# Gates of both layers and the even layer's queries and keys computed by token and turned by 16-bit DMA transposes

## The chip, the cores and the metric

The kernel runs on one core of a Trainium2 chip. A core has five engines, each of which works off its own queue of instructions in order: TensorE (PE in the profile; PEld is its weight loading), VectorE (DVE), ScalarE (ACT), GpSimd (POOL) and SyncE (SP), which here only issues DMAs. Sixteen DMA engines move the data. The metric is the device time of one execution in microseconds (us), the median over several runs.

## The reference, cut to what matters

Two residual layers work on 256 tokens of width 2048; a last RMS norm follows. Each layer normalises, projects, attends in sixteen heads of 128 features, multiplies by a SiLU gate, projects back and adds.

```python
for layer in (even_layer, odd_layer):
    x = x + layer(rms_norm(x, g_layer))
return rms_norm(x, g_final)

def even_layer(y):
    qa, ka, va, ga, qb, kb, vb, gb = _split(y @ w_in, EVEN_SPLITS)
    oa = dilated_attention(qa, ka, va, bias_a)
    ob = neighbourhood_attention(qb, kb, vb, rpb_b)
    mix = concatenate([oa * silu(ga), ob * silu(gb)])
    return mix @ w_out
```

The odd layer has the same frame. Its heads C (eight, with a sink logit) have queries, two key and value heads and gates; its heads D (eight) normalise and rotate queries and keys, and have two key and value heads too. The logits of a head are the product of its queries and keys over the 128 features, so both are wanted with the features on the partitions.

## The kernel before

Every float32 product is made of three products of halves, hi x hi, hi x lo and lo x hi, summed in PSUM. The input `X` lies in SBUF as 16 slices of 128 features, each split into hi and lo. The weights are 268 tiles of 128x1024 (512 KB), read once each in the order of the list `plan`. The class `Weights` (L54 to L74) loads a tile into one of five raw buffers (L65, issued by SyncE), ScalarE casts it to `whi` (L69) and VectorE makes the rest `wlo` (L70); there are three pairs of `whi` and `wlo`. `weights()` (L78) keeps two tiles ahead of TensorE.

A unit of work is a group of weight tiles that share one result in PSUM. It has two forms.

- By feature (L275): the weights are stationary and the input streams through. A tile holds four slices of 256 features; each slice takes two matmuls of 512 columns (L284) and two of 256 (L288). A unit is four tiles and gives 256 features, features on the partitions. To evict it ScalarE copies one half out of PSUM, VectorE adds the other and multiplies by the row scale of the norm, which `spread_scale` (L187) has laid along the columns.
- By token (L294): the input is stationary and the weights stream, in three matmuls a slice (`mm3`, L100). A unit is eight tiles of two slices and gives 512 features, tokens on the partitions; with 256 features it is four tiles of four slices.

Before the change the queries, keys and gates of the even layer (24 units), and the gates, the C queries and the first keys of the odd layer (13 units) are made by feature. Values and the D heads are made by token; the D heads are turned by TensorE after their rotation (`normed_rope`, L362).

The order of the work is set by Python generators. `step()` (L216) is called once a weight tile and moves each list of generators on by one: `evac` (evictions), `post` (rotation) and `bg` (attention). `attend` (L423) does two heads: logits, exponentials, the turning of the probabilities, weighing of the values, in about ten steps. The turning (L475 to L492) goes by 16-bit halves: GpSimd parts the words into halves (L480), two DMA transposes turn them (L482), GpSimd joins them (L491). DMAs given to `pinned` (L85) keep their place in program order. SyncE issues all DMAs in order, so that a DMA which waits holds up those behind it. `ROOM` (L205) says how many queries, keys, gates and bias tables may live at once. Seven constants of `load_consts` (L144) are loaded while the second pair of heads is under way. `project_out` works through the output weights by `out_order` (L561).

Of the kernel before, what the change touches and what calls it, by code (L numbers as in the profile page):

```python
# [36 lines left out]
def encoder(ctx, tc, a, out):  # L37
# [37 lines left out]

    plan, ready = [], []
# [102 lines left out]
    def row_scale(layer, parts):  # L179
# [5 lines left out]
        return r  # L185

    def spread_scale(r):  # L187
# [28 lines left out]
    def step():  # L216

        advance(evac)
        advance(post)
        attention()  # L220
# [16 lines left out]
    def drain():  # L237
        while evac or post or bg:
            step()
# [15 lines left out]
    steps = {}  # L255

    def need(pr):

        while pr not in done:
            assert evac or post or bg  # L260
# [101 lines left out]
    def normed_rope(tag, q, ss, g, scale, give):  # L362
# [21 lines left out]
        yield  # L384
        yield from room(tag)
# [7 lines left out]
        yield  # L393

# [28 lines left out]
    def attend(idx, q, kv, silu, frees, bias=None, sink=None, shared=False):  # L423

        (qh, ql), (kh, kl), (vh, vl, v0) = q, kv[0], kv[1]
# [100 lines left out]
        yield  # L526
        o = ps_o.tile([P, 2, S], F32, tag="o", name="ps_out")
# [4 lines left out]
        yield True  # L532
        m = tp.tile([P, 2, S], F32, tag="tmp", name="mx", bufs=4)
# [426 lines left out]
```

## Time and profile before

| What | Before |
|---|---|
| Median of 3 runs | 817.8 us (817.39 to 818.31) |
| Profiled execution, its span | 817.19 us, 815.4 us |
| TensorE's granted clock | 0.997 |
| TensorE busy | 805.6 us, 99% |
| VectorE, ScalarE, GpSimd busy | 577.7, 447.8, 128.6 us |
| DMA | 168.47 MB, 207 GB/s |

How to read it: matmuls overlap in the array, and the modelled end of one lies beyond the start of the next, so the duration of a matmul is not what it costs; its cost is read from start to start in the timeline. Idle time of an engine that nobody waits for costs nothing. A wait for several things is put down to the one that ended last.

### The profile page before, as it was taken

What the parts mean: (1) busy time and instruction counts of PE and PEld (TensorE: products, weight loads), DVE (VectorE), ACT (ScalarE), POOL (GpSimd) and SP (SyncE); (2) the same over time, 40 slices, a digit from 0 to 9 for tenths busy, and PEclk for the clock granted to TensorE, in tenths of its full rate; (3) what the DMA queues carried; (4) which work ended last, traced back from release to release, by engine and by line L of the source; (5) the groups of instructions that cost most, each with busy time, mean ns of one, the idle gap of its engine ahead of it and who ended that gap; (6) DMA issues with size and microseconds to landing.
All of it is one profiled execution on the core that took longest, in us unless ns stands there. A gap on an engine that the chain in (4) does not pass through costs nothing.

```text
span 815.4 us, 11762 instructions
## 1 busy us (share of the span) xinstructions
PE 805.6 (99%) x4293; PEld 691.7 (85%) x4293; DVE 577.7 (71%) x855; ACT 447.8 (55%) x712; POOL 128.6 (16%) x100
## 2 busy tenths in 40 slices
PE   9999999999999999999999999999999999999996
PEld 7888888888888888888888888888889888888885
DVE  6677676677857887497656776685987776765863
ACT  7755454555545554455445555657656665664651
POOL 0002020021302240040204300002112223221000
PEclk9999999999999999999999999999999999999998
DMA  9957675565755756566758755566558676767632
GB/s 337 362 200 221 250 228 181 207 206 175 235 176 171 231 164 245 186 186 222 203 184 194 253 198 166 197 203 201 153 179 231 221 213 186 235 196 227 206 133 103
DMA packets 97066, 168.47 MB, mean 207 GB/s; under 512 B 55472, under 2 KB 56368, under 8 KB 96944
## 3 DMA queue, kind: packets, MB, share of 16 engines
q1 hardware_dynamic: 96864, 167.71, 64.3%
q8 instruction: 33, 0.54, 0.3%
q14 instruction: 25, 0.20, 0.1%
q10 hardware_dynamic: 144, 0.02, 0.0%
HBM read 155.64 MB, written 3.05 MB: 195 GB/s over the span
## 4 chain that ended last, share of the span: by engine, by line
PE 98%; DMA 1%; DVE 0%; SPq 0%; ACT 0%; issue 0%; ACTq 0%; DVEq 0%
PE ps_f L284 34%; PE ps_f L288 17%; PE ps_t L103 14%; PE ps_t L104 14%; PE ps_t L102 13%; PE ps_s L104 1%; PE ps_s L103 1%; PE ps_s L102 1%; PE ps_out L103 1%; PE ps_out L102 1%; PE ps_out L104 1%; DMA wraw<-in_even_t 1%; SPq L87 0%; PE ps_tr L389 0%; DVE wlo L70 0%; ACT whi L69 0%
## 5 line engine op out<-in xcount | busy, mean ns | idle before, releaser
L70 DVE TENSOR_TENSOR wlo<-wraw,whi 128x1024 fp32r<-128x1024 f32 (+1 forms) x270 | 346.3, 1283 | 184.6 <-ACT whi L69 183.3
L69 ACT CAST whi<-wraw 128x1024 fp32r<-128x1024 f32 (+1 forms) x270 | 282.2, 1045 | 300.2 <-PE ps_t L104 127.8
L284 PE MATMUL ps_f<-x,whi 128*128 128x512 f32 x1184 | 372.1, 396 | 0.0
L288 PEld LDWEIGHTS ps_f<-x,wlo 128*128 128x128 f32 x1184 | 222.2, 188 | 53.5 <-DVE wlo L70 1.2
L288 PE MATMUL ps_f<-x,wlo 128*128 128x256 f32 x1184 | 233.0, 278 | 0.0
L284 PEld LDWEIGHTS ps_f<-x,whi 128*128 128x128 f32 x1184 | 180.8, 189 | 0.5
L102 PE MATMUL ps_t<-whi,x 128*128 128x512 f32 (+1 forms) x256 | 96.3, 379 | 0.6 <-ACT x L95 0.5
L103 PE MATMUL ps_t<-wlo,x 128*128 128x512 f32 (+1 forms) x256 | 96.1, 377 | 0.1
L104 PE MATMUL ps_t<-whi,x 128*128 128x512 f32 (+1 forms) x256 | 95.9, 377 | 0.0
L480 POOL COPY ph<-pr 128x1024 uint16<-128x1024 uint16 x32 | 39.5, 1235 | 350.8 <-ACT pr L470 182.9
L102 PE MATMUL ps_t<-whi,mh 128*128 128x512 f32 x240 | 93.5, 389 | 0.0
L103 PE MATMUL ps_t<-wlo,mh 128*128 128x512 f32 x240 | 93.5, 389 | 0.0
L104 PE MATMUL ps_t<-whi,ml 128*128 128x512 f32 x240 | 93.4, 389 | 0.0
L491 POOL COPY pt<-pa 128x1024 uint16<-128x1024 uint16 x32 | 51.5, 1608 | 35.8 <-DMA pa<-ph 35.8
L102 PEld LDWEIGHTS ps_t<-whi,x 128*128 128x128 f32 x256 | 48.2, 188 | 9.6 <-ACT x L95 1.3
L104 PEld LDWEIGHTS ps_t<-whi,x 128*128 128x128 f32 x256 | 48.2, 188 | 9.0 <-DVE x L96 0.2
L103 PEld LDWEIGHTS ps_t<-wlo,x 128*128 128x128 f32 x256 | 48.2, 189 | 8.6 <-DVE wlo L70 0.5
L104 PEld LDWEIGHTS ps_t<-whi,ml 128*128 128x128 f32 x240 | 45.1, 188 | 9.3
L102 PEld LDWEIGHTS ps_t<-whi,mh 128*128 128x128 f32 x240 | 45.1, 188 | 9.2
L103 PEld LDWEIGHTS ps_t<-wlo,mh 128*128 128x128 f32 x240 | 45.1, 188 | 9.1
L420 POOL TENSOR_TENSOR bias<-maskB,rpb 128x512 f32<-128x512 f32 x8 | 12.2, 1526 | 137.6 <-DMA rpb<-rows 137.6
L462 ACT ACTIVATE pr<-lg,mn 128x256 f32<-128x256 f32 (+1 forms) x48 | 24.0, 501 | 16.8 <-POOL ph L480 9.2
(133 smaller groups left out, 675.5 us busy)
## 6 DMA issues: line engine op xcount, KB each, us to landing
wraw<-in_even_f SPq DMA_DIRECT2D x96, 512.0 KB, 3.4
wraw<-in_odd_f SPq DMA_DIRECT2D x56, 512.0 KB, 3.6
wraw<-in_w_out_even SPq DMA_DIRECT2D x32, 512.0 KB, 4.1
wraw<-in_w_out_odd SPq DMA_DIRECT2D x32, 512.0 KB, 4.2
wraw<-in_even_t SPq DMA_DIRECT2D x30, 512.0 KB, 4.3
wraw<-in_odd_t SPq DMA_DIRECT2D x24, 512.0 KB, 3.4
xraw<-in_xt SPq DMA_DIRECT2D x8, 256.0 KB, 7.0
h<-in_x SPq DMA_DIRECT2D x4, 512.0 KB, 8.6
```

The source lines that it names most:

```text
L69: nc.scalar.copy(self.hi[:, c], raw[:, c])
L70: nc.vector.tensor_sub(self.lo[:, c], raw[:, c], self.hi[:, c].bitcast(F32))
L102: nc.tensor.matmul(dst, lh, rh, start=first, stop=False, skip_group_check=True)
L103: nc.tensor.matmul(dst, lh, rl, start=False, stop=False, skip_group_check=True)
L104: nc.tensor.matmul(dst, ll, rh, start=False, stop=last, skip_group_check=True)
L284: nc.tensor.matmul(acc[:, f, :], w.hi[:, c], xx[k], start=k == 0, stop=False, skip_group_check=True)
L288: nc.tensor.matmul(acc[:, f, :S], w.lo[:, c], xh[k], start=False, stop=k == KC - 1, skip_group_check=True)
L420: nc.gpsimd.tensor_tensor(b, maskB.unsqueeze(1).to_broadcast([P, 2, S]), raw, op=ALU.subtract)
L462: nc.scalar.activation(p[:, t, :W], lg[:, t, :W], AF.Exp, bias=mn[:, t : t + 1], scale=-1.0, accum_out=den[:, t : t + 1],)
L480: nc.gpsimd.tensor_copy(halves, words)
L491: nc.gpsimd.tensor_copy(words.bitcast(U16).rearrange("p c (q s) -> p s c q", s=2), st[i])
```

## The change

Queries and keys of the even layer, the gates of both layers, and the first keys of the odd layer are computed by token, 512 features a unit; the first odd keys share a unit with the first odd values. `side_by_side` fills a weight tile from two groups of 256 features: two DMAs, each with two runs of 1 KB a partition. `EVEN` gives the order of the even units: a digit is queries and keys of one pair of heads, `g` the gates of two pairs, `v` their values.

ScalarE scales the pieces by the row scale while it copies them from PSUM (`evict_turned`, `evict_gates`). GpSimd parts the words into halves, two DMA transposes turn them, GpSimd joins them; queries and keys are then split into hi and lo. For gates, Tanh and the product come before the turning, and the joined words are the gate. The queues `later` and `jobs` are moved on by `step()`. Attention begins when the keys are given, and waits for values and gates where it uses them. The spread scale stays for the C queries alone, which are still made by feature.

```diff
+            if isinstance(src, list):
+                for place, piece in src:
+                    nc.sync.dma_start(place(raw), piece)
             for i, c in enumerate(cols):
                 load = nc.sync.dma_start if x is None else pinned
-                load(raw[:, c], src[:, c])
+                if not isinstance(src, list):
+                    load(raw[:, c], src[:, c])
...
+    def side_by_side(left, right):
+        for j in range(NJ):
+            pieces = []
+            for i, group in enumerate((left, right)):
+                place = lambda raw, i=i: raw.rearrange("p (k c) -> p k c", k=KK)[:, :, i * S : (i + 1) * S]
+                src = group[j // 2].rearrange("p (k c) -> p k c", c=S)
+                pieces.append((place, src[:, j % 2 * KK : (j % 2 + 1) * KK]))
+            plan.append((pieces, None))
...
+        half, minus = [const.tile([P, 2], F32, tag=f"{x}{layer}", name=f"{x}{layer}") for x in ("half", "minus")]
+        nc.vector.tensor_scalar_mul(half, r, 0.5)
+        nc.vector.tensor_scalar_mul(minus, r, -SCALE)
+        return r, half, minus
...
-        rk = const.tile([P, S], F32, tag="rk", name="rk")
         rq = const.tile([P, S], F32, tag="rq", name="rq")
-        nc.vector.tensor_copy(rk, bc)
-        nc.vector.tensor_scalar_mul(rq, rk, -SCALE)
-        rhalf = const.tile([P, S], F32, tag="rhalf", name="rhalf")
-        nc.vector.tensor_scalar_mul(rhalf, rk, 0.5)
-        return rk, rq, rhalf
-    evac, post, bg, done = [], [], [], set()
+        nc.vector.tensor_scalar_mul(rq, bc, -SCALE)
+        return rq
...
+        turn(later)
+        turn(jobs)
...
-    def gate(acc, rhalf):
-        g = scaled(acc, rhalf)
-        e = tp.tile([P, 2, S], F32, tag="ge", name="ge", bufs=1)
-        nc.scalar.activation(e, g, AF.Tanh)
+    def evict_gates(acc, half, pairs):
+        for i, pr in enumerate(pairs):
+            g = tp.tile([P, 2, S], F32, tag="tmp", name="gf", bufs=4)
+            for t in range(2):
+                nc.scalar.mul(g[:, t, :], acc[t][:, i * S : (i + 1) * S], half[:, t : t + 1])
+            later.append(gate(g, pr))
+            steps[id(later[-1])] = 0
+            yield
+    def gate(g, pr):
+        e = tp.tile([P, 2, S], F32, tag="ge", name="ge")
+        tc.keep_in_program_order(nc.scalar.activation(e, g, AF.Tanh))
+        nc.vector.scalar_tensor_tensor(g, e, 1.0, g, ALU.add, ALU.mult)
+        yield
+        halves = tp.tile([P, 2, 2, S], U16, tag="ge", name="gh")
+        tc.keep_in_program_order(
+            nc.gpsimd.tensor_copy(halves, g.bitcast(U16).rearrange("p t (k s) -> p t s k", s=2))
+        )
+        yield
+        across = g.rearrange("p t k -> p (t k)").bitcast(U16).rearrange("p (s c q) -> p s c q", s=2, c=2)
+        for t in range(2):
+            pinned(
+                across[:, :, :, t * P : (t + 1) * P].rearrange("p s c q -> p (s c) q"),
+                halves[:, t].rearrange("p s k -> p (s k)"), transpose=True,
+            )
+        yield
+        yield
+        yield
+        yield from room("silu")
         s = silu_tile()
-        nc.vector.scalar_tensor_tensor(s, e, 1.0, g, ALU.add, ALU.mult)
-        return s
+        tc.keep_in_program_order(
+            nc.gpsimd.tensor_copy(s.bitcast(U16).rearrange("p c (q s) -> p s c q", s=2), across)
+        )
+        yield
+        gated[pr] = s
+        yield
+    def evict_turned(acc, parts):
+        for i, (tag, scale, give) in enumerate(parts):
+            f = tp.tile([P, 2, S], F32, tag="tmp", name="tf", bufs=4)
+            for t in range(2):
+                nc.scalar.mul(f[:, t, :], acc[t][:, i * S : (i + 1) * S], scale[:, t : t + 1])
+            jobs.append(turned(f, tag, give))
+            steps[id(jobs[-1])] = 0
+            yield
+    def turned(f, tag, give):
+        words = tp.tile([P, 2, S], F32, tag="tmp2", name="tw")
+        halves, across = [
+            x.rearrange("p t k -> p (t k)").bitcast(U16).rearrange("p (x y z) -> p x y z", x=2, y=2) for x in (words, f)
+        ]
+        pin(nc.gpsimd.tensor_copy(halves, f.bitcast(U16).rearrange("p t (k s) -> p t s k", s=2)))
+        yield
+        for t in range(2):
+            pinned(
+                across[:, :, :, t * P : (t + 1) * P].rearrange("p s c q -> p (s c) q"),
+                halves[:, t].rearrange("p s k -> p (s k)"), transpose=True,
+            )
+        yield
+        yield
+        yield
+        pin(nc.gpsimd.tensor_copy(words.bitcast(U16).rearrange("p c (q s) -> p s c q", s=2), across))
+        yield
+        yield from room(tag)
+        dst = pair(tag)
+        split(*dst, words, None, pin)
+        yield
+        give(dst)
...
+            vh, vl, v0 = kv[1]()
...
+        while held or kv[1]() is None:
+            yield
+        held.append(idx)
...
+        while idx not in gated:
+            yield True
         m = tp.tile([P, 2, S], F32, tag="tmp", name="mx", bufs=4)
-        nc.vector.tensor_mul(m, o, silu)
+        pin(nc.vector.tensor_mul(m, o, gated.pop(idx)))
...
-    def even_order(u):
-        tokens, first = [(None, "v")], [(0, "q"), (0, "k")]
-        head = tokens + first if u == 0 else first + tokens
-        return head + [(0, "g"), (1, "q"), (1, "k"), (1, "g")]
+    EVEN = ["v 0 g 1", "g 0 v 1", "g 0 v 1", "0 1 v g"]
     for u in range(4):
-        for pr, kind in even_order(u):
+        for kind in EVEN[u].split():
             if kind == "v":
                 plan.extend((a["even_t"][u][j], None if u else j) for j in range(8))
+            elif kind == "g":
+                side_by_side(a["even_f"][2 * u][2], a["even_f"][2 * u + 1][2])
             else:
-                plan.extend((a["even_f"][2 * u + pr]["qkg".index(kind)][j], None) for j in range(4))
+                side_by_side(*(a["even_f"][2 * u + int(kind)][i] for i in range(2)))
     out_plan("even")
     for t, fs in ((0, ()), (1, (10, 11)), (2, (12, 13))):
         plan.extend((a["odd_t"][t][j], None) for j in range(8))
-        plan.extend((a["odd_f"][f][j], None) for f in fs for j in range(4))
-    plan.extend((a["odd_f"][f][j], None) for f in (0, 1, 2, 6, 3, 7, 4, 8, 5, 9) for j in range(4))
+        if fs:
+            side_by_side(*(a["odd_f"][f] for f in fs))
...
+    def evict_even(u, kind, acc):
+        r, half, minus = scales[0]
         if kind == "v":
-            values(st["v"], acc, r)
-        elif kind == "q":
-            st["q"] = scaled_split("q", acc, rq)
+            tiles = values_tile()
+            values(tiles, acc, r)
+            yield
+            yield
+            v[u] = tiles
+        elif kind == "g":
+            yield from evict_gates(acc, half, (2 * u, 2 * u + 1))
+        else:
+            p, st = 2 * u + int(kind), {}
             heads = (2 * (p % 4), 2 * (p % 4) + 1)
-            st["bias"] = [bias_table(a["bias_a"][x]) if p < 4 else bias_rpb(x) for x in heads]
-        elif kind == "k":
-            st["k"] = scaled_split("k", acc, rk)
-        else:
-            s = gate(acc, rhalf)
-            v = (*st["v"], p % 2 * S)
-            bg.append(attend(p, st["q"], (st["k"], v), s, ("q", "k", "silu", "bias", "bias"), st["bias"]))
+            bias = [bias_table(a["bias_a"][x]) if p < 4 else bias_rpb(x) for x in heads]
+            def begin(dst):
+                bg.append(attend(p, st["q"], (dst, lambda: u in v and (*v[u], p % 2 * S) or None), ("q", "k", "silu", "bias", "bias"), bias))
+            yield from evict_turned(acc, [("q", minus, lambda dst: st.__setitem__("q", dst)), ("k", r, begin)])
...
+    def evict_odd(i, acc, st):
+        st["q", i] = scaled_split("q", acc, scales[1])
+        st["bias", i] = [bias_table(a["bias_c"][x]) for x in (2 * i, 2 * i + 1)]
+        yield
+        yield
+        while "k" not in st:
+            yield
+        attend_odd(0, i, st)
+        yield
+    def gate_pairs(first):
+        evac.append(evict_gates(by_token(512, token_acc()), half1, (first, first + 1)))
     st = {}
     acc = by_token(512, token_acc())
     evac += [evict_heads(st, ("k", None), acc), evict_values(part(acc, 1), 1)]
     for i in (0, 2):
         evac.append(evict_heads(st, (("q", i), ("q", i + 1)), by_token(512, token_acc())))
-        for m in range(2):
-            evac.append(evict_odd(1, "g", i + m, by_feature(), st))
+        gate_pairs(4 + i)
     st = {}
-    evac.append(evict_odd(0, "k", 0, by_feature(), st))
-    evac.append(evict_values(part(by_token(S, token_acc()), 0), 0))
+    acc = by_token(512, token_acc())
+    evac += [evict_turned(acc, [("k", r1, lambda dst: st.__setitem__("k", dst))]), evict_values(part(acc, 1), 0)]
     for i in range(4):
-        for kind in "qg":
-            evac.append(evict_odd(0, kind, i, by_feature(), st))
+        evac.append(evict_odd(i, by_feature(), st))
+        if i % 2 == 0:
+            gate_pairs(i)
```

TensorE's queue around the first logits of the even layer, before (`ps_f` is a unit by feature, `ps_s` the logits):

```order
L284 MATMUL ps_f_708<-x0_87,whi_665 128x512 x2
L288 MATMUL ps_f_708<-x0_87,wlo_666 128x256 x2
L102 MATMUL ps_s_739<-kh_634,qh_599 128x256
L103 MATMUL ps_s_739<-kl_635,qh_599 128x256
L104 MATMUL ps_s_739<-kh_634,ql_600 128x256
```

The same place after the change (`ps_t` is a unit by token):

```order
L118 MATMUL ps_t_748<-whi_706,x0_87 128x512
L119 MATMUL ps_t_748<-wlo_707,x0_87 128x512
L120 MATMUL ps_t_748<-whi_706,x0_87 128x512
L118 MATMUL ps_s_774<-kh_744,qh_701 128x256
L119 MATMUL ps_s_774<-kl_745,qh_701 128x256
L120 MATMUL ps_s_774<-kh_744,ql_702 128x256
```

Three matmuls of 512 columns a slice stand where two of 512 and two of 256 stood; the logits are the same, and stand four tiles later.

SyncE's queue around the constants, before (`pa` probabilities being turned, `wraw` weight tiles, `rows`, `maskB` and `cosT` the first of the constants):

```order
L87 DMA_TRANSPOSE pa_836<-ph_835 128x4x128 x2
L65 DMA wraw_940<-in_even_f 128x1024
L87 DMA_TRANSPOSE pa_884<-ph_883 128x4x128 x2
L65 DMA wraw_965<-in_even_f 128x1024
L65 DMA wraw_1002<-in_even_f 128x1024
L65 DMA wraw_1030<-in_even_f 128x1024
L65 DMA wraw_1056<-in_even_f 128x1024
L65 DMA wraw_1079<-in_even_f 128x1024
L87 DMA rows_134<-in_rpb_b 64x3720
L87 DMA maskB_130<-in_mask_b 128x256
L87 DMA cosT_128<-in_cos 128x256
```

The same place after the change (`gf` gates being turned, `bias` two tables of the attention's bias):

```order
L103 DMA_TRANSPOSE gf_768<-gh_807 128x4x128 x2
L66 DMA wraw_935<-in_even_f 128x2x256 x2
L103 DMA_TRANSPOSE pa_874<-ph_873 128x4x128 x2
L66 DMA wraw_960<-in_even_f 128x2x256 x2
L103 DMA_TRANSPOSE gf_804<-gh_871 128x4x128 x2
L103 DMA_TRANSPOSE pa_908<-ph_907 128x4x128 x2
L66 DMA wraw_984<-in_even_f 128x2x256 x2
L103 DMA bias_1003<-in_bias_a 128x512
L103 DMA bias_1005<-in_bias_a 128x512
L103 DMA rows_134<-in_rpb_b 64x3720
L103 DMA maskB_130<-in_mask_b 128x256
L103 DMA cosT_128<-in_cos 128x256
```

Eight transposes stand where four stood, and between the last of them and the constants the load of one weight tile where five stood. Four more constants follow, and then the load of tile 35, `wraw_1028`.

## Rows read from the trace of the kernel before

**Rows 1.** The page: engines' busy time, and the chain that ended last.

```profile
PE 805.6 (99%) x4293; PEld 691.7 (85%) x4293; DVE 577.7 (71%) x855; ACT 447.8 (55%) x712; POOL 128.6 (16%) x100
...
PE 98%; DMA 1%; DVE 0%; SPq 0%; ACT 0%; issue 0%; ACTq 0%; DVEq 0%
```

**Rows 2.** Waits: who waited for whom; us in total, times, longest.

```profile
ACT whi L69 <- DMA wraw<-in_even_f: 4.9, 4, 2.3
...
PEld ps_f L288 <- DVE wlo L70: 1.2, 3, 0.4
```

**Rows 3.** Timeline of TensorE, by feature: start, us, engine, line, matmul, count.

```profile
69.15 0.63 PE L284 MATMUL ps_f<-x,whi 128*128 128x512 f32 x2
...
88.66 0.28 PE L102 MATMUL ps_out<-pth,vh 128*128 128x256 f32 x1
```

**Rows 4.** Timeline of TensorE, five tiles by token.

```profile
226.31 0.39 PE L102 MATMUL ps_t<-whi,x 128*128 128x512 f32 x1
...
239.91 0.61 PE L284 MATMUL ps_f<-x,whi 128*128 128x512 f32 x2
```

**Rows 5.** Timeline of TensorE, four 256-wide tiles of the first odd values.

```profile
604.08 0.28 PE L102 MATMUL ps_t<-whi,x 128*128 128x256 f32 x1
...
615.60 0.63 PE L284 MATMUL ps_f<-x,whi 128*128 128x512 f32 x2
```

**Rows 6.** ScalarE and VectorE by line: busy us, mean ns; splits' min/median/max.

```profile
L69 ACT CAST whi<-wraw 128x1024 fp32r<-128x1024 f32 x266 | 279.7, 1052 | 297.8 <-PE ps_t L104 127.8 <-PE ps_f L284 108.1 <-issue 35.1
L327 ACT COPY qf<-ps_f 128x512 f32<-128x512 f32 x37 | 21.4, 577 | 0.0
L355 ACT ACTIVATE rq<-ps_t,rstd 128x256 f32<-128x256 f32 x10 | 4.4, 469 | 0.0
...
L328 DVE TENSOR_TENSOR qf<-ps_f,qf 128x512 f32<-128x512 f32 x37 | 25.3, 682 | 0.0
...
L70 DVE TENSOR_TENSOR wlo<-wraw,whi x270: 691/1226/2316, 4.6 to 789.6; 128x1024 fp32r<-128x1024 f32 x133, 128x512 fp32r<-128x512 f32 x2
```

**Rows 7.** Waits of SyncE, the DMA queue's own.

```profile
SPq L65 <- DVE wlo L70: 418.8, 191, 5.8
...
SPq L87 <- POOL ph L480: 26.1, 24, 2.4
```

**Rows 8.** DMA issues: count, KB each, median us from issue to landing.

```profile
wraw<-in_even_f SPq DMA_DIRECT2D x96, 512.0 KB, 3.4
...
sink<-in_sinks_c SPq DMA_DIRECT2D x1, 4.0 KB, 7.5
```

**Rows 9.** GpSimd by line: the two 16-bit copies around a transpose.

```profile
L491 POOL COPY pt<-pa 128x1024 uint16<-128x1024 uint16 x32 | 51.5, 1608 | 35.8 <-DMA pa<-ph 35.8
L480 POOL COPY ph<-pr 128x1024 uint16<-128x1024 uint16 x32 | 39.5, 1235 | 350.8 <-ACT pr L470 182.9 <-DVE pr L472 159.1 <-ACT whi L69 8.8
```

**Rows 10.** Two stretches: length, busy PE PEld DVE ACT POOL, clock, DMA share, GB/s.

```profile
580.00:600.00 20.00, 19.99 (x119) 17.08 (x118) 19.80 (x36) 12.45 (x22) 5.42 (x4) 1.00 0.60 175
20.00:40.00 20.00, 19.98 (x103) 16.75 (x102) 11.90 (x16) 14.53 (x29) 0.00 (x0) 1.00 0.98 363
```

**Rows 11.** Timeline of SyncE: transposes, then the constants and the load behind.

```profile
70.30 2.60 SPq L87 DMA_TRANSPOSE pa<-ph  x2
...
85.81 0.61 SPq L87 DMA_DIRECT2D rows<-in_rpb_b  x1
...
90.17 8.18 SPq L65 DMA_DIRECT2D wraw<-in_even_f  x4
98.40 0.90 SPq L87 DMA_DIRECT2D bias<-in_bias_a  x2
100.80 0.33 SPq L65 DMA_DIRECT2D wraw<-in_even_f  x1
```

**Rows 12.** Timeline of SyncE: three of the four loads of an rpb table.

```profile
204.76 1.91 SPq L87 DMA_DIRECT2D rpb<-rows  x3
```

**Rows 13.** Timeline: the first lo half by feature.

```profile
28.82 0.30 PEld L288 LDWEIGHTS ps_f<-x,wlo 128*128 128x128 f32 x2 [0.45 <-DVE wlo L70]
```

More of the change, by code (lines that the diff above doesn't have):

```diff
@@ L237, in drain @@
     def drain():
-        while evac or post or bg:
+        while evac or post or later or jobs or bg:
             step()
@@ L253, in turning, with turn @@
             turns.pop(0)
-    steps = {}
+    steps, jobs = {}, []
+    def turn(queue):
+        for i, job in enumerate(list(queue)):
+            if i and steps[id(queue[i - 1])] < 3 or i > 1:
+                break
+            steps[id(job)] += 1
+            try:
+                next(job)
+            except StopIteration:
+                steps[id(job)] = 99
+        while queue and steps[id(queue[0])] == 99:
+            steps.pop(id(queue.pop(0)))
     def need(pr):
         while pr not in done:
-            assert evac or post or bg
+            assert evac or post or later or jobs or bg
             step()
@@ L360, in heads_by_token, with normed_rope @@
         return q, ss
-    def normed_rope(tag, q, ss, g, scale, give):
+    def normed_rope(tag, q, ss, g, scale, give, begin):
         rr = sm.tile([P, 4], F32, tag="drr", name="drr")
@@ L421, in bias_rpb, with attend @@
         return b
-    def attend(idx, q, kv, silu, frees, bias=None, sink=None, shared=False):
-        (qh, ql), (kh, kl), (vh, vl, v0) = q, kv[0], kv[1]
+    def attend(idx, q, kv, frees, bias=None, sink=None, shared=False):
+        (qh, ql), (kh, kl) = q, kv[0]
         kvh = lambda i: kv[2] if shared else i
@@ L585, in encoder @@
         plan.extend((a["odd_t"][t][j], None) for j in range(8))
-        plan.extend((a["odd_f"][f][j], None) for f in fs for j in range(4))
-    plan.extend((a["odd_f"][f][j], None) for f in (0, 1, 2, 6, 3, 7, 4, 8, 5, 9) for j in range(4))
+        if fs:
+            side_by_side(*(a["odd_f"][f] for f in fs))
+    for fs in ((0, 1), (2,), (6, 7), (3,), (4,), (8, 9), (5,)):
+        if len(fs) == 2:
+            side_by_side(*(a["odd_f"][f] for f in fs))
+        else:
+            plan.extend((a["odd_f"][fs[0]][j], None) for j in range(4))
     out_plan("odd")
@@ L632, in encoder @@
     for u in range(4):
-        st = {}
         if u == 1:
             bg.append(later_consts())
-        for pr, kind in even_order(u):
-            if kind != "v":
-                evac.append(evict_even(2 * u + pr, kind, by_feature(), st))
-                continue
-            if u:
+        for kind in EVEN[u].split():
+            if u or kind != "v":
                 acc = by_token(512, token_acc())
@@ L730, in part, with attend_odd @@
         return [x[:, i * S : (i + 1) * S] for x in acc]
-    def attend_odd(branch, i, st, s):
+    def attend_odd(branch, i, st):
         frees = ["q", "silu"] + ["bias", "bias"] * (branch == 0) + ["k"] * (i == 3)
-        kv, heads = (st["k"], (*v, (1 - branch) * S), i // 2), (2 * i, 2 * i + 1)
+        kv, heads = (st["k"], lambda: (*v, (1 - branch) * S), i // 2), (2 * i, 2 * i + 1)
         bg.append(
-            attend(4 * branch + i, st["q", i], kv, s, frees, st.get(("bias", i)), heads if branch == 0 else None, True)
+            attend(4 * branch + i, st["q", i], kv, frees, st.get(("bias", i)), heads if branch == 0 else None, True)
         )
@@ L750, in evict_heads @@
                 give = lambda dst, key=key: st.__setitem__(key, dst)
-                post.append(normed_rope("k" if key == "k" else "q", q, ss, g, scale, give))
+                begin = (lambda: None) if key == "k" else lambda key=key: attend_odd(1, key[1], st)
+                post.append(normed_rope("k" if key == "k" else "q", q, ss, g, scale, give, begin))
             yield
-    def when_ready(i, st, s):
-        attend_odd(1, i, st, s)
+    def evict_odd(i, acc, st):
+        st["q", i] = scaled_split("q", acc, scales[1])
+        st["bias", i] = [bias_table(a["bias_c"][x]) for x in (2 * i, 2 * i + 1)]
         yield
-    def evict_odd(branch, kind, i, acc, st):
-        rk, rq, rhalf = scales[1]
-        if kind == "k":
-            st["k"] = scaled_split("k", acc, rk)
-        elif kind == "q":
-            st["q", i] = scaled_split("q", acc, rq)
-            st["bias", i] = [bias_table(a["bias_c"][x]) for x in (2 * i, 2 * i + 1)]
-        else:
-            s = gate(acc, rhalf)
-            if branch:
-                post.append(when_ready(i, st, s))
-            else:
-                attend_odd(branch, i, st, s)
-        yield
+        yield
+        while "k" not in st:
+            yield
+        attend_odd(0, i, st)
+        yield
+    def gate_pairs(first):
+        evac.append(evict_gates(by_token(512, token_acc()), half1, (first, first + 1)))
     st = {}
```

20 lines of the change are left out of this document (9 added, 11 removed).

## The prediction

> **What bounds the kernel now.** I read the page's first and fourth parts first. TensorE is busy 805.6 of 815.4 us, and 98% of the chain that ended last is matmuls [rows 1]: the time is the length of the matmul stream, and the other engines matter only where they make it wait. So the second view was the list of waits for TensorE and its weight loads. In the whole run its weight loads by feature waited 1.2 us for a lo half, and ScalarE's casts 4.9 us, in four waits, for such tiles' loads [rows 2]. VectorE (577.7 us busy) and ScalarE (447.8 us) have room on average, GpSimd (128.6 us) has most [rows 1].
>
> Third I read the matmul stream itself, start to start, since the durations of matmuls overlap. Seven weight tiles by feature run without a break from 69.15 to 88.66 us: 19.51 / 7 = 2.787 us a tile [rows 3]. Five tiles by token run from 226.31 to 239.91 us: 13.60 / 5 = 2.720 us [rows 4]. Both tiles push the same 6,144 columns (8 x 512 + 8 x 256 against 12 x 512). By feature there are 16 weight loads and matmuls for them, by token 12, and the shorter list is 0.067 us faster. The four 256-wide tiles of the first odd values take 11.52 us, 2.88 a tile [rows 5]. So the more matmuls for the same columns, the slower.
>
> Last I read how far ahead the weights are. ScalarE casts a tile when TensorE gives a buffer back (three pairs of hi and lo): 1.05 us, then 1.23 us of VectorE [rows 6], so a pair is ready about 2.3 us after the end of tile i-3, while TensorE wants it two tiles (5.4 us) later. That is 3.1 us of cover. The load can go out when one of five raw buffers is free. SyncE waits 418.8 us for just that [rows 7], so loads are early: wanted 13.6 us after tile i-8 ends, free 2.3 us after it, 3.4 us in flight [rows 8]; 7.9 us of cover. A load may be 7.9 + 3.1 = 11 us late before TensorE stops.
>
> **The change part by part.** *Matmuls.* 24 feature units of the even layer and eight odd gate units become 16 token units of eight tiles: 128 tiles x 0.067 = -8.6 us. First odd keys (4 x 2.787) and values (4 x 2.88) become one token unit (8 x 2.720): 22.67 - 21.76 = -0.9 us. Two small transposes that spread the first scale go too; I leave them out. Sum -9.5 us, all of it on the path.
>
> *Evictions.* The order shows 33 pieces that lose a ScalarE copy (0.577 us) and VectorE's add (0.682) and its multiply, which has the add's shape and gets the same price, and gain two scaled copies on ScalarE (0.469 each, the shape that the rotary heads have today) and two 16-bit copies on GpSimd (the two rows of that shape: 1.2 and 1.6 us) [rows 6, 9]. VectorE: -33 x 1.36 = -45 us. ScalarE: 33 x (0.94 - 0.58) = +12 us. GpSimd: 33 x 2.85 = +94 us, to some 223 of about 812. All three stay below 70% busy and beside TensorE, so I price them at nothing. If a GpSimd copy stretches a VectorE split by up to 1.1 us (1.2 us is usual, 2.3 the longest [rows 6]), 66 of them make at most 72 us in a column that has just lost 45. It would show only where VectorE is full, as at 580 to 600 us (19.80 of 20), and even there TensorE lost 0.01 us [rows 10].
>
> *SyncE's queue.* It gets 66 more transposes, issued in 1.3 us each (two take 2.6 [rows 11]): 86 us. 136 weight loads become two half loads with 1 KB runs. Each issue is 0.33 us if it costs what a load does now [rows 11], 0.6 if the number of pieces counts, as it may for the rpb loads (three take 1.91 [rows 12]): 45 to 118 us more. Waits for the copy before a transpose (26.1 us in 24 waits today, 1.1 each [rows 7]) come to about 36 us for 33 pairs. Together 167 to 240 us out of 418.8 that the queue now spends waiting for free buffers: it fits on average. The question is bunches. Pinned pieces cannot be passed, and a load behind them is late by their sum.
>
> The longest bunch is in the first round. From the first gate transpose to the load of tile 35 the queue holds eight transposes (10.4 us), three tiles of loads (2.0 to 3.6), two bias tables (0.9) and the seven constants (85.81 to 90.17, 4.4 us; all in [rows 11]): 17.7 to 19.3 us. The first of them can go when gate halves exist: the gate unit is tiles 16 to 23, and behind the cast of tile 26, which starts as tile 23 ends, come two scaled copies and one of the next piece, Tanh, VectorE's product and GpSimd's copy: 1.05 + 1.41 + 0.58 + 0.68 + 1.24 = 5.0 us (Tanh and product priced as the copy and the add of their shape), with the hand-overs about 5.4, that is when tile 25 ends. So load 35 goes out 17.7 to 19.3 us after the end of tile 25. Its buffer was free 2.3 us after the end of tile 27, 7.7 us after that of tile 25: it is 10.0 to 11.6 us late. It also lands late, behind the constants: the last of those takes 7.5 us against 3.4 [rows 8], +4.1. Lateness 14.1 to 15.7 us against 11 us of cover, to which the two bursts of weighing in between (12 matmuls of 0.12 us as in [rows 5], 1.4) add: 12.4. Stall 1.7 to 3.3 us; bounds 0 (transposes start a tile earlier) to 7 (each pair waits 1.1 us for its copy). I take 3.0. Today that batch does no harm, since few transposes stand ahead of it and the load left at 90.17, one tile into that cover.
>
> Four more bunches of eight transposes (second and third even pairs of heads, odd gates twice) lack the constants: 12.4 to 14.0 us from the first transpose to the load behind it, whose buffer was free 5.0 us after that first transpose: 9.0 us late at most against 11, so nothing.
>
> *Opening.* Around 20 to 40 us the DMA engines are full (0.98 busy, 363 GB/s [rows 10]) and the first feature tile is waited for: the weight load of its first lo half waited 0.45 us for VectorE's split [rows 13]. By token the lo half is wanted at the second matmul, not at the third: +0.23 us (2.720 / 12). The 1 KB runs have no row. From below 0, since the bytes are the same; from above a tile at half the rate, 0.52 MB / 363 GB/s = 1.4 us. I take a quarter, since these DMAs share the queue with 2 KB runs already; together +0.6 (0.2 to 1.7).
>
> *The rest.* Attention keeps its instructions. A head pair now starts four to eight tiles later in the even layer, but the last pair needs its output at the same place as before, and no wait in the order is forced there. The waits move from values to gates, and a gate is due about ten tiles after its unit ends.
>
> *Sum.* -9.5 + 3.0 + 0.6 = -5.9 us. The profiled execution took 817.19 us (span 815.4 and 1.8 around it), so 811.3; the runs' median, 817.8, lies 0.6 above it: **811.9 us**.
>
> **Rivals.**
> *A, the whole gain:* the constants' batch does not stall, because the first gate transposes leave a tile earlier or the constants land faster. Then -9.5 + 0.6 with at most 0.5 us from the VectorE waits that go: 808 to 809. For it: casts seldom wait for loads today [rows 2]. Against it: the count above.
> *B, slower, columns alone set the pace:* if a tile cost what its columns cost, both forms would take the same and the matmul term would be nothing: 817.8 + 3.6 = 821.4. It decides from the first even unit on. Against it stand [rows 3 and 4], 2.787 against 2.720 for equal columns, and the 256-wide ones in [rows 5]. The Trainium skill (TensorE: Matmul & The Clock Gate, Back-to-back issue gap) says that a warm matmul costs N / 2.4 ns and 2.5 ns more; by that figure the whole change would save an estimated 1.4 us in matmuls and the sum would be 820. The trace has 227 ns for 512 columns where that rule has 216 [rows 4], so by that rule neither form is explained and I hold to the rows.
> *C, slower, SyncE's queue:* every pair of transposes in the five bunches waits for its GpSimd copy as long as the mean wait today, 1.1 us. Four pairs make 4.4 us; the four lighter bunches have 2.0 us to spare, so each stalls 2.4 (+9.6), and the first 4.4 more: 811.9 + 14.0 = 825.9. It decides where the waits in a bunch pass 2.0 us. For it: loads and transposes stand in one line. Against it: every GpSimd copy is issued a step of 2.7 us ahead of its transposes, and the longest such wait today is 2.4 us [rows 7].
> *D, in between:* two or three such stalls, 814.5 to 820.
> That the change does not do what it says is excluded by the order: 768 of each token matmul where 224 stood (and 32 narrow ones), 128 of each feature matmul where 1,184 stood.
>
> **How the numbers follow.** Forecast (809.5 to 814.5) 0.50, A 0.17, D 0.14, B 0.06, C 0.13. A measurement of this kernel tells 0.2%, 1.6 us, from no change: within 816.2 to 819.4 is the same. Forecast and A are faster, 0.67, and about a third of D, 0.05: 0.72. Same: 0.06 of D and 0.02 of B where it is partly true: 0.08. Slower: C, the rest of B and of D: 0.20. The range runs from 806.5, the whole gain with no cost in the opening and no VectorE waits, to 818.5, past most of D; C and B lie beyond. The likeliest case's own range is 809.5 to 814.5.
>
> **What would show it.** Token tiles of the former feature units at 2.72 us in the matmul timeline, and a TensorE busy time near 797 us plus stalls. The stall of the first round as a wait of ScalarE's cast for a weight load, at about 105 to 112 us, and of TensorE for a lo half behind it. ScalarE's waits for weight loads elsewhere near nothing, SyncE's waits for free buffers fallen by about half. GpSimd near 223 us, VectorE near 530. I am wrong if token tiles run at 2.78 or more in the new units, if ScalarE waits for loads at several bunches, or if TensorE waits for logits' queries and keys.

## The result and the profile after

The changed kernel takes 822.65 us (median; 821.94 to 824.22) against 817.68 us of the kernel before in the same runs: 1.0061 times as long, 95% interval 1.0048 to 1.0073. The forecast was 811.9 us, in a range of 806.5 to 818.5. It was wrong: the kernel became slower by 5 us, not faster by 6.

The page of the changed kernel, its engines and its chain, beside [rows 1]:

```profile
PE 800.5 (97%) x3715; PEld 664.4 (81%) x3715; DVE 553.8 (67%) x786; ACT 453.6 (55%) x745; POOL 231.2 (28%) x166
...
PE 76%; DMA 8%; SPq 5%; POOL 4%; DVE 3%; issue 2%; ACT 1%; ACTq 0%; POOLq 0%; DVEq 0%
```

TensorE is busy 5 us less in a span that is 5.7 us longer, and the chain, 98% matmuls before, now runs a fifth of its way through DMA, SyncE, GpSimd and VectorE. The kernel is no longer bound by matmuls alone.

The gain in matmuls did arrive. TensorE's timeline in the queries and keys of the third pair of heads, every twelfth matmul (start, us, engine, line, matmul, count):

```profile
132.30 0.39 PE L120 MATMUL ps_t<-whi,x 128*128 128x512 f32 x1
...
135.02 0.39 PE L120 MATMUL ps_t<-whi,x 128*128 128x512 f32 x1
...
137.74 0.39 PE L120 MATMUL ps_t<-whi,x 128*128 128x512 f32 x1
```

A tile takes 2.72 us, as forecast, where it took 2.787 in [rows 3]. I added up the whole stream for both kernels, each matmul at its own undisturbed distance to the next (227 ns by token, 233.3 and 115.4 by feature, 120 for 256 columns in attention): 802.0 us before, 792.5 after. That is the forecast's -9.5 us. What the true starts have above this sum are stalls: 4.1 us before, 18.4 after. With 0.9 us more between the last instruction of an engine and the end of the span, these make up the profiled difference: -9.5 + 14.3 + 0.9 = 5.7.

The stalls stand in two places: 2.9 us at 105 to 108 us, and 10.0 us at 317 to 370 us. The other 1.4 us is in small pieces. The first, in ScalarE's timeline and then TensorE's (brackets: idle before, and what ended it):

```profile
105.67 1.04 ACT L74 CAST whi<-wraw 128x1024 fp32r<-128x1024 f32 x1 [7.57 <-DMA wraw<-in_even_f]
```
```profile
104.79 0.39 PE L120 MATMUL ps_t<-whi,x 128*128 128x512 f32 x1
106.77 0.51 PE L118 MATMUL ps_t<-whi,x 128*128 128x512 f32 x1 [1.59 <-ACT whi L74]
108.03 0.50 PE L119 MATMUL ps_t<-wlo,x 128*128 128x512 f32 x1 [0.75 <-DVE wlo L75]
```

A cast waits 7.57 us for its load, and TensorE waits for that cast and for the split behind it: the first-round stall as forecast, at the place and near the size (3.0).

The second is in the last quarter of the even layer, where the units of pairs of heads 5, 6 and 7 (counted from 0) follow one another, and in the values behind them. SyncE's waits from 300 to 356 us (who waited for whom: us, times, longest):

```profile
SPq L103 <- POOL tw L427: 5.8, 2, 3.5
SPq L103 <- DMA rpb<-rows: 4.3, 4, 2.1
SPq L103 <- POOL bias L518: 3.4, 2, 1.9
...
SPq L66 <- DVE wlo L75: 0.2, 1, 0.2
```

Its wait for a free raw buffer, the queue's slack, is 0.2 us in 56: SyncE is behind all the time. In 13.5 us it stands at a pinned rpb load or transpose. (In the kernel before, the waits for a free buffer were 37.2 us in the 60 us from 300 us on, and TensorE waited for nothing there.) The timelines of SyncE and GpSimd show how that hangs together:

```profile
331.84 2.59 SPq L103 DMA_DIRECT2D rpb<-rows  x4
334.53 1.02 SPq L70 DMA_DIRECT2D wraw<-in_even_t  x2
340.89 2.57 SPq L103 DMA_DIRECT2D rpb<-rows  x4
343.50 1.08 SPq L70 DMA_DIRECT2D wraw<-in_even_t  x2
348.14 5.15 SPq L103 DMA_TRANSPOSE tf<-tw  x4
353.39 0.53 SPq L70 DMA_DIRECT2D wraw<-in_even_t  x1
```
```profile
338.98 1.88 POOL L518 TENSOR_TENSOR bias<-maskB,rpb 128x512 f32<-128x512 f32 x1 [2.64 <-DMA rpb<-rows]
345.70 1.43 POOL L518 TENSOR_TENSOR bias<-maskB,rpb 128x512 f32<-128x512 f32 x1 [4.84 <-DMA rpb<-rows]
347.09 2.48 POOL L427 COPY tw<-tf 128x1024 uint16<-128x1024 uint16 x2
```

Both rpb tables of a pair of heads (neighbourhood bias) pass through one raw buffer. SyncE issues the first table's loads; GpSimd waits for them and subtracts; only then can SyncE issue the second table's loads (5.3 us stood still, 335.6 to 340.9); GpSimd waits for those too, and the 16-bit copies of the queries and keys stand behind that on GpSimd, with the transposes on SyncE behind the copies (3.5 us more). From 331.84 to 353.39, eight tiles' time on TensorE, four tiles were loaded.

TensorE's weight loads in the stretch from 290 to 375 us then wait mostly for the split of a late tile:

```profile
PEld ps_t L119 <- DVE wlo L75: 7.1, 7, 2.1
```

### The profile page after: what moved, and what is told of

It is laid out like the page before. It is cut to its first block, busy times and chain, and to the rows that moved or that the text cites. A ratio compares the mean times of both kernels' runs of the same rounds, so it can differ in the third digit from the quotient of the medians.

```text
span 821.1 us, 11035 instructions
## 1 busy us (share of the span) xinstructions
PE 800.5 (97%) x3715; PEld 664.4 (81%) x3715; DVE 553.8 (67%) x786; ACT 453.6 (55%) x745; POOL 231.2 (28%) x166
## 3 DMA queue, kind: packets, MB, share of 16 engines
HBM read 155.64 MB, written 3.05 MB: 193 GB/s over the span
## 4 chain that ended last, share of the span: by engine, by line
PE 76%; DMA 8%; SPq 5%; POOL 4%; DVE 3%; issue 2%; ACT 1%; ACTq 0%; POOLq 0%; DVEq 0%
PE ps_t L119 22%; PE ps_t L120 22%; PE ps_t L118 22%; SPq L103 4%; PE ps_f L314 4%; DMA rpb<-rows 2%; DMA wraw<-in_even_f 2%; PE ps_f L318 2%; DVE wlo L75 2%; DMA pa<-ph 1%; POOL pt L589 1%; POOL ph L578 1%; SPq L66 1%; DMA wraw<-in_even_t 1%; DMA rows<-in_rpb_b 1%
## 5 line engine op out<-in xcount | busy, mean ns | idle before, releaser
L75 DVE TENSOR_TENSOR wlo<-wraw,whi 128x1024 fp32r<-128x1024 f32 (+1 forms) x270 | 356.5, 1321 | 209.7 <-ACT whi L74 204.6
L119 PE MATMUL ps_t<-wlo,x 128*128 128x512 f32 x768 | 300.1, 391 | 6.2 <-DVE wlo L75 6.1
L118 PE MATMUL ps_t<-whi,x 128*128 128x512 f32 x768 | 300.3, 392 | 3.8 <-ACT whi L74 3.0
L120 PE MATMUL ps_t<-whi,x 128*128 128x512 f32 x768 | 298.6, 389 | 0.0
L119 PEld LDWEIGHTS ps_t<-wlo,x 128*128 128x128 f32 x768 | 144.2, 188 | 37.8 <-DVE wlo L75 10.0
L118 PEld LDWEIGHTS ps_t<-whi,x 128*128 128x128 f32 x768 | 144.2, 188 | 35.7 <-ACT whi L74 5.1
L120 PEld LDWEIGHTS ps_t<-whi,x 128*128 128x128 f32 x768 | 144.2, 188 | 30.3 <-DVE x L112 0.2
L578 POOL COPY ph<-pr 128x1024 uint16<-128x1024 uint16 x32 | 44.8, 1400 | 123.5 <-DVE pr L570 62.2
L390 POOL COPY gh<-gf 128x1024 uint16<-128x1024 uint16 x16 | 19.9, 1241 | 151.1 <-DVE gf L386 135.3
L427 POOL COPY tw<-tf 128x1024 uint16<-128x1024 uint16 x17 | 21.9, 1310 | 68.3 <-ACT tf L416 68.3
L314 PE MATMUL ps_f<-x,whi 128*128 128x512 f32 x128 | 40.2, 395 | 0.0
L598 DVE TENSOR_TENSOR ptl<-pt,pth 128x512 fp32r<-128x512 f32 x32 | 31.5, 989 | 6.7 <-ACT pth L597 6.7
L437 POOL COPY tw<-tf 128x1024 uint16<-128x1024 uint16 x17 | 26.5, 1566 | 23.0 <-DMA tf<-tw 23.0
```

Of the source, the lines that this page charges most:

```text
L75: nc.vector.tensor_sub(self.lo[:, c], raw[:, c], self.hi[:, c].bitcast(F32))
L118: nc.tensor.matmul(dst, lh, rh, start=first, stop=False, skip_group_check=True)
L119: nc.tensor.matmul(dst, lh, rl, start=False, stop=False, skip_group_check=True)
L120: nc.tensor.matmul(dst, ll, rh, start=False, stop=last, skip_group_check=True)
L314: nc.tensor.matmul(acc[:, f, :], w.hi[:, c], xx[k], start=k == 0, stop=False, skip_group_check=True)
L437: pin(nc.gpsimd.tensor_copy(words.bitcast(U16).rearrange("p c (q s) -> p s c q", s=2), across))
```

## The experiments

Two theories were told apart. **W (waits):** pinned DMAs that wait for GpSimd hold up the weight loads. **S (sum):** SyncE simply has too much to issue. "Stalls" below are the sum of TensorE's starts above the undisturbed stream, as worked out above. They belong to the one profiled execution, whose time stands beside them and can lie off the median by up to 3.7 us; "us" is the median, with the ratio to the kernel before in the same runs.

| Kernel | us | Ratio (95%) | Profiled us | Stream | Stalls |
|---|---|---|---|---|---|
| before | 817.7 | 1 | 817.19 | 802.0 | 4.1 |
| changed | 822.65 | 1.0061 (1.0048 to 1.0073) | 823.17 | 792.5 | 18.4 |
| no rpb | 814.56 | 0.9960 (0.9949 to 0.9972) | 813.85 | 792.5 | 9.3 |
| tables early | 814.62 | 0.9959 (0.9947 to 0.9971) | 812.79 | 792.5 | 7.7 |
| constants spread | 819.60 | 1.0029 (1.0016 to 1.0042) | 817.61 | 792.5 | 12.8 |
| one load | 817.49 | 0.9995 (0.9979 to 1.0011) | 821.22 | 792.5 | 16.5 |
| two raw buffers | 813.06 | 0.9956 (0.9943 to 0.9968) | 815.26 | 792.5 | 10.3 |
| gates only | 817.21 | 0.9993 (0.9985 to 1.0002) | 817.17 | 796.9 | 8.3 |
| gates, constants spread | 815.45 | 0.9969 (0.9956 to 0.9981) | 815.90 | 796.9 | 7.0 |
| both edits | 810.36 | 0.9910 (0.9895 to 0.9924) | 810.91 | 792.5 | 5.9 |
| both and one load | 810.72 | 0.9916 (0.9904 to 0.9929) | 810.52 | 792.5 | 5.9 |
| both, quarter loads | 831.69 | 1.0178 (1.0161 to 1.0194) | 831.05 | 792.5 | 26.3 |

In four of these executions a part of the stalls is matmuls at a lower granted clock and not waiting: 1.6 us each in no rpb, one load and two raw buffers, 4.2 us with quarter loads (by the distances of the matmuls; see the last section).

**No rpb.**

```diff
-            bias = [bias_table(a["bias_a"][x]) if p < 4 else bias_rpb(x) for x in heads]
+            bias = [bias_table(a["bias_a"][x]) for x in heads]
```

> The changed kernel without the neighbourhood bias: the pairs of heads 4 to 7 of the even layer take the other heads' ready tables (one load of 512 KB a pair in two DMAs) in place of four small rpb loads and a GpSimd subtraction for each table. It leaves out the rpb gather and its mask. Theory W (waits: SyncE stands at rpb loads and transposes that wait for GpSimd, which itself waits for the rpb loads, and the weight loads behind come late): the stalls of TensorE at 317 to 370 us, 9.9 us together, go: 812.7 us (811.5 to 814.5), the stall at 105 to 108 us of 2.9 us stays. Theory S (sum: SyncE has too many DMAs to issue in that round, transposes and two half loads a tile, whether they wait or not): 16 issues of 0.62 us go and 4 of 0.45 come, 8.1 us less over two units, so part of the stalls goes: 815 to 819.

814.56 us: 8.1 less than the changed kernel, and no stall from 290 to 375 us. That is 0.06 above W's range and below S's. The rpb chain makes the second stall. It doesn't tell waits from issues, since both went.

**Tables early, step by step.**

```diff
+            if u > 1 and kind in "01":
+                tables.append(spread_rpb(2 * u + int(kind)))
...
+        yield
+        yield
+        yield from room("bias")
         take("bias")
```

> The changed kernel with the rpb loads of a pair of heads begun one unit (eight tiles) earlier and its two tables made step by step, so that no rpb load, no subtraction and no transposes stand directly behind one another. The same instructions and the same number of DMAs as the changed kernel. Theory W: the stalls at 317 to 370 us go, 812.7 us (811.5 to 815). Theory S: the same issue time in the same units, so 820 to 823. The stall at 105 to 108 us stays in both.

814.62 us, 8.0 less, with every rpb load still there. SyncE's waits in the stretch from 290 to 356 us:

```profile
SPq L70 <- DVE wlo L75: 6.0, 4, 2.1
SPq L66 <- DVE wlo L75: 3.6, 4, 1.7
SPq L103 <- POOL tw L428: 1.9, 2, 1.4
...
SPq L103 <- POOL bias L529: 0.7, 1, 0.7
```

9.6 us of slack (waits for a free raw buffer) are back in these 66 us, 9.2 of them from 300 us on, and the pinned waits for tables and copies fell from 9.2 us to 2.6. TensorE loses nothing there. Full DMA engines, the other way for a load to be late, are not the cause: they were 0.86 busy from 290 to 346 us here, and 0.75 from 300 to 356 us in the changed kernel. So the waits were the cause, as W has it. The profiled execution, 812.79 us, is at W's middle value. The other four took 814.51 to 815.60 us, at a mean granted clock of 0.995 against its 0.997; no trace shows what they lost.

**Constants spread.** Each constant is followed by two steps, the first at tile 40.

```diff
-        if u == 1:
-            bg.append(later_consts())
+            if (u, kind) == (1, "0"):
+                slow.append(later_consts())
```

> The changed kernel with the seven constants loaded one every two tiles, from tile 40 on, in place of all at once before the load of tile 35. If the constants' batch makes the first stall (105 to 108 us, 2.9 us): 819.8 us (819 to 820.8), the stalls at 317 to 370 us unchanged. If the eight transposes ahead of it alone make that stall: no change, 822.6.

819.60 us, 3.05 less, though its eleven runs go from 817.53 to 823.10 us. Between 84 and 112 us no cast waits for a load any more; the constants' batch was the first stall, the eight transposes alone cost nothing.

**One load a tile.** `side_by_side` takes whole tiles, laid out beside each other in DRAM.

```diff
...
-                pieces.append((place, src[:, j % 2 * KK : (j % 2 + 1) * KK]))
-            plan.append((pieces, None))
+        plan.extend((a[left][right][j], None) for j in range(NJ))
```

> The changed kernel with the side-by-side tiles laid out whole in DRAM, so that each is one DMA of 512 KB with 4 KB runs and not two with 1 KB runs: 136 issues of about 0.45 us less on SyncE, 61 us in all, some 3.6 us a unit. Theory S: the stalls at 317 to 370 us shrink by the issue time of some 13 tiles, 6 us, and the first by 1 to 2: 813 to 816. Theory W: SyncE's waits for GpSimd hang on the rpb loads' landing and stay: 819 to 822, with at most 1 us from the opening.

817.49 us, between both theories, and spread over 813.71 to 821.22; the changed kernel's four runs spread over 2.3 us, those with constants spread over 5.6. Its profile shows the slowest of its executions, with both stalls still there (1.8 and 9.5 us). It decided nothing: the median is 5.2 us below the changed kernel's, so less to issue helps a queue that is late, and how much varies from one execution to the next.

**Two raw buffers.**

```diff
-        raw = tp.tile([P, 2, S], F32, tag="rpb", name="rpb", bufs=1)
+        raw = tp.tile([P, 2, S], F32, tag="rpb", name="rpb", bufs=2)
```

> The changed kernel with two buffers in place of one for the raw rpb rows (room made by dropping a tile of ones and one small buffer of the scale's spreading). The rpb loads keep their places, but the second table's four loads no longer wait for the first table's subtraction. Theory W: of SyncE's waits for GpSimd at 309 to 348 us (2.0, 1.5, 5.3 and 3.5 us) the first and the third go and the others shorten, so most of the 9.9 us goes: 814 to 817. Theory S (issue time alone): nothing changes, 821 to 823.

813.06 us, 9.6 less and 0.9 below W's range: nearly the whole second stall, of which 0.3 us is left in the trace. The order of the rpb loads on SyncE is that of the changed kernel, and in the stretch of the stall the edit takes out only this one kind of wait. (What made room for the buffer, and the turned input of the odd layer, which has two of these buffers now as well, lie outside that stretch.) SyncE stands at no rpb load from 300 to 356 us any more; its waits for the copies of queries and keys fell from 5.8 us to 3.5. This settles which wait it was: that of the second table's loads for the first table's subtraction. The slack there is still small, 1.3 us, and it is enough.

**Gates only.** Queries and keys by feature again, gates and first odd keys by token.

```diff
...
+            if kind in "01":
+                for which in "qk":
+                    evac.append(evict_even(u, kind + which, by_feature()))
+                continue
```

> The change for the gates of both layers and the first odd keys alone: queries and keys of the even layer are again computed by feature, so GpSimd and SyncE have no queries and keys to turn there. Matmuls by the traces: 64 gate tiles x 0.067 and 0.9 for keys and values, 5.2 us less than before. Theory W: no piece stands behind the rpb tables, and only four gate transposes before the constants, so no stalls: 817.8 - 5.2 = 812.6 (811.5 to 814.5). Theory S: 34 pairs of transposes and 64 tiles of half loads go, so no stalls either; the same. If the gates' turning were itself a cost: 816 or more.

817.21 us, 4.6 above what I expected. The stream is 5.1 us shorter, as expected, but stalls are 4.2 more than in the kernel before: 1.8 at the constants, 0.7 at logits that now wait for their keys' lo half (attention begins a step too soon in this kernel), 0.5 around 585 us, and 1.0 in the first 30 us, which I don't lay to the edit, since the other five kernels run with it or after it show it too (4.5 to 5.0 us there, against some 3.7 in the kernel before); all six ran on other chips than the four runs made before them. The expectation had missed the constants: fewer transposes stand ahead of them here, and they stall all the same.

**Gates, constants spread.** The edit of the constants added to it.

> Gates of both layers and the first odd keys by token, queries and keys of the even layer by feature, and the constants loaded one every two tiles. In the kernel with the gates alone the trace shows stalls of 1.8 us around 105 us and some 0.7 us at logits that wait for their keys' lo half. If the constants make the first here too: 817.2 - 1.8 = 815.4 (814.5 to 816.3). If the gates' turning makes it: 817.2.

815.45 us, as expected: with half of the change, too, the constants make a stall.

**Both edits, and both with one load.** Tables early and constants spread together; then whole tiles as well.

> The changed kernel with rpb tables made a unit earlier step by step, and with the constants loaded one every two tiles. Both stalls should go: 814.6 - 3.0 = 811.6 (810.5 to 812.7); by the first prediction's sum without its 3.0 us of stall, 808.9.

> The same two edits and one load of 512 KB for each side-by-side tile. If half loads cost only through SyncE's lateness, nothing is left to gain: 811.6 as with the two edits. If the opening or a landing suffers from 1 KB runs: 0.3 to 1.5 us less, 810.1 to 811.3.

810.36 us, 0.1 below its range, and 810.72 us: both beat the kernel before, by 0.9%, and each other by nothing. The second lies where whole loads were to help, but that range was set against 811.6; against 810.36 they gain nothing. Two loads of 1 KB runs cost nothing as long as SyncE has slack. The page of the kernel with both edits:

```profile
PE 797.4 (99%) x3715; PEld 666.9 (82%) x3715; DVE 557.3 (69%) x786; ACT 454.0 (56%) x745; POOL 233.6 (29%) x166
...
PE 95%; DVE 2%; DMA 1%; ACT 1%; issue 0%; ACTq 0%; SPq 0%; DVEq 0%
```

TensorE is 99% busy and the chain is matmuls again.

**Quarter loads.** The kernel with both edits, but four DMAs a side-by-side tile.

```diff
-                pieces.append((place, src[:, j % 2 * KK : (j % 2 + 1) * KK]))
+                for m in range(KK):
+                    at = lambda raw, place=place, m=m: place(raw)[:, m : m + 1]
+                    pieces.append((at, src[:, j % 2 * KK + m : j % 2 * KK + m + 1]))
```

> The kernel with both edits (tables early and step by step, constants spread), but each side-by-side tile loaded by four DMAs of 128 KB, not two of 256 KB: 272 issues more on SyncE, by 0.45 us each 122 us, 7.2 us a unit, with no new wait for GpSimd. A unit of eight tiles lasts 21.8 us, and SyncE then issues 8 transposes (10.4 us) and 8 tiles x 1.8 (14.4 us), 24.8 us, and 5.2 us more where rpb tables are loaded. Theory S (the queue's issue time): TensorE stalls in the even layer's units of pairs of heads, 816 to 830 us. Theory W (waits for GpSimd alone make lateness): no stalls, 810 to 812 us.

831.69 us, 21.3 more and 1.7 above S's range, without any new wait for GpSimd. From 290 to 345 us SyncE waits for 2.6 us in all, 0.3 of them for a free buffer. The smaller loads do not land later: 3.1 us after issue at their median, against 4.2 for the half loads of the kernel with both edits. So S holds as well, and W as "waits alone" falls. SyncE is one queue with one budget, 21.8 us a unit of eight tiles; issue time and waits draw on it alike. In the changed kernel issues took about two thirds of the 56 us from 300 us on, and the waits took nearly all the rest.

## Why the prediction was wrong

**Right:** the matmul term (-9.5 forecast, -9.5 in the stream), so rival B falls although its time, 821.4, is the nearest of all. The rule beside it, from the Trainium skill (TensorE: Matmul & The Clock Gate, Back-to-back issue gap), gave an estimated 1.4 us for this term; the trace disagrees, with 9.5 us. Right too: the first-round stall (3.0 forecast, 2.9 in the trace, 3.05 by the run without it), in place and in cause. That the size fits to 0.1 us is in part luck, since the same place loses 4.3 us in the trace without rpb and 3.6 with two raw buffers, where a lower clock comes on top. Right as well: GpSimd's time (223 forecast, 231.2); and that the evictions' work hides beside TensorE. The opening was to cost 0.6: in the first 30 us the stalls of the two kernels agree within 0.2 us, and whole loads gained nothing later, so it cost next to nothing. VectorE lost 24 us and not 45, which nobody waits for.

**Wrong:** the step "Four more bunches of eight transposes (second and third even pairs of heads, odd gates twice) lack the constants: ... 9.0 us late at most against 11, so nothing". The stall it put at nothing cost 10.0 us. Its list left the last quarter of the even layer out, and its count held transposes and weight loads only. There the queue has 16 rpb loads as well (some 10 us of issue at 0.61 us each), and three pairs of heads in a row with no unit of values or gates between them. Above all "Attention keeps its instructions" was taken to mean that its DMAs keep their price. The rpb tables were free in the kernel before. There GpSimd waits for their loads longer than for nearly anything else (its list of waits: us, times, longest); most of that time lies before the loads were issued, since they land 2.2 to 3.9 us after issue. Nothing that was due soon stood behind:

```profile
POOL bias L420 <- DMA rpb<-rows: 137.6, 8, 43.7
```

The change put the copies of queries and keys behind those waits, and SyncE's transposes behind the copies. What was added was cheap; what it was queued behind was not. One of the prediction's own signs of being wrong came with it: ScalarE waits for such tiles' loads in 19 places, 37.2 us, where it was 4 and 4.9 us before [rows 2].

The same two-table chain runs in the third quarter, for pairs 4 and 5, with 16 rpb loads. There other units lie between the pairs, SyncE still has 8.2 us of waits for a free buffer from 215 to 300 us, and TensorE loses nothing. That is why one stretch alone pays. Over the whole run SyncE's waits for free buffers fell to about half, as forecast, from 418.8 us [rows 7] to 226.1:

```profile
SPq L70 <- DVE wlo L75: 131.4, 67, 3.8
SPq L66 <- DVE wlo L75: 94.7, 69, 3.3
```

Half of the slack was left on average and next to none (0.2 us) where it was needed.

Rival C had the right engine and the right kind of wait, but put 2.4 us on each of four bunches and 4.4 more on the first (825.9). None of the bunches that it names stalled beyond the constants.

What stays open: the output's last DMAs land 0.8 us later after the last engine instruction in all eleven kernels with the change (here 820.06 - 815.85 = 4.2 us against 814.51 - 811.10 = 3.4); no run tells why.

## What to carry to other kernels

When work is added to an in-order queue that loads also use, add up what the queue does in the time of a unit, issues and waits together, for every unit and not only for the one that looks worst; the slack to draw on is the queue's own wait for free buffers in that stretch. Ask of each added instruction what it stands behind on its engine: an old wait that cost nothing becomes the price of whatever is put behind it. A second buffer, or an earlier start in steps, may give back what seemed the cost of the change itself.

## What was not expected of the hardware

After some of TensorE's waits its granted clock fell to the lower of its two levels, 1.2 and 2.4 GHz. In the kernel with quarter loads it waited 2.98 us and then 0.77 us at 312 to 314 us. A little later its matmuls stand 0.43 us apart where they stand 0.23 apart otherwise, and the granted clock from 315 to 317 us is 0.50 of full. After a wait of 4.04 us the same happens at once:

```profile
312.33 0.49 PE L120 MATMUL ps_t<-whi,x 128*128 128x512 f32 x1 [2.98 <-ACT whi L74]
...
315.07 0.63 PE L120 MATMUL ps_t<-whi,x 128*128 128x512 f32 x1
315.50 0.63 PE L121 MATMUL ps_t<-wlo,x 128*128 128x512 f32 x1
...
318.04 0.40 PE L121 MATMUL ps_t<-wlo,x 128*128 128x512 f32 x1
318.27 0.40 PE L122 MATMUL ps_t<-whi,x 128*128 128x512 f32 x1
...
339.83 0.80 PE L120 MATMUL ps_t<-whi,x 128*128 128x512 f32 x1 [4.04 <-ACT whi L74]
```

In ten-microsecond stretches of that kernel (length, busy PE, PEld, DVE, ACT, POOL, granted clock, DMA share, GB/s):

```profile
320.00:330.00 10.00, 10.00 (x52) 8.47 (x51) 6.59 (x16) 5.77 (x14) 5.72 (x5) 1.00 0.79 211
...
340.00:350.00 10.00, 9.54 (x32) 7.31 (x32) 6.79 (x8) 6.60 (x10) 1.34 (x1) 0.73 0.82 299
```

The granted clock is 0.73 of full in the last, a mean of the two levels: at 0.227 us such a stretch holds 44 of these matmuls, and here it holds 32 with 0.5 us idle. So a stall can be paid for again in slow matmuls, 4.2 of this kernel's 26.3 us.

The length of a wait alone does not tell whether the clock falls. At the first stall the changed kernel waited 1.59 and 0.75 us and stayed at 1.00 from 109 to 112 us; the kernel without rpb waited 1.42 and 0.76 us and stood at 0.50 there, the one with two raw buffers 0.87 and 0.76 us, at 0.51. A wait of 1.81 us at 365 us in the kernel with one load was followed by 0.50 (367 to 370 us), one of 2.26 us at 336 us with constants spread by nothing (1.00 from 333 to 345 us). What decides it, no run here shows.

The splits of probabilities on VectorE (`ptl`), 0.68 us at their median in both kernels, reach 1.80 us at most in the changed one against 0.69 before. The Trainium skill (SBUF — State Buffer, Terms) says that VectorE and GpSimd take turns at one pair of ports, held for a whole instruction. The trace agrees with taking turns: all eleven of the 32 splits that take over 0.70 us overlap a copy or a subtraction on GpSimd, as the one from 142.50 to 144.29 us overlaps a copy from 141.47 to 143.80, and none without such an overlap takes longer than that. Three that overlap one are not longer. The splits of weights do the same: without an overlap none takes over 1.23 us in either kernel. In all `ptl` takes 31.5 us where it took 21.5, and `wlo` 356.5 where it took 346.3: 20 us more, about what VectorE's gain fell short of the forecast (24 against 45).
